# An encoder on one core: sums of down weights beside the output projection, operands kept and stored later, the residual stream in DRAM, another cast order

## The chip, the core and the metric

The kernel runs on one core of a Trainium2 chip. The core has five engines that run at the same time, each through its own list of instructions in order: TensorE (PE, matrix multiplies into PSUM, with its weight loads shown as PEld), VectorE (DVE), ScalarE (ACT), GpSimd (POOL) and SyncE (SP), which issues all the DMAs of this kernel. SBUF is the on-chip memory, PSUM holds the sums of matmuls, and DRAM holds inputs, outputs and scratch. Engines wait for each other by semaphores. The metric is the device time of one execution in microseconds (us); less is better.

## The reference

Two sequences, a prompt of 256 tokens and a sample of 512, go through the same two-layer encoder of width 1024. The first layer mixes with an mLSTM that runs in both directions, the second with sliding-window attention; each is followed by an FFN whose hidden rows are convolved along the sequence.

```python
def conv_ffn(h, w_up, conv_w, conv_b, w_down):
    u = h @ w_up
    u = lax.conv_general_dilated(u, conv_w[:, None, :], ...) + conv_b
    g = u[..., :D_FF]
    val = u[..., D_FF:]
    return (jax.nn.silu(g) * val) @ w_down

def trunk(x, c, ...):
    for l in range(DEPTH):
        mod = jax.nn.silu(c) @ adaln_w[l] + adaln_b[l]
        sh1, sc1, g1, sh2, sc2, g2 = ...
        h = rmsnorm(x, norm_g[l, 0]) * (1 + sc1) + sh1
        y = mlstm_mixer(...) if l % N_MIXERS == 0 else swa_mixer(...)
        x = x + g1 * y
        h = rmsnorm(x, norm_g[l, 1]) * (1 + sc2) + sh2
        x = x + g2 * conv_ffn(h, ffn_w_up[l], ffn_conv_w[l], ffn_conv_b[l], ffn_w_down[l])
    return rmsnorm(x, final_g)
```

D_FF is 2816. Everything is in float32.

## The kernel before

**Layout.** Both sequences stand side by side as T = 768 columns (the prompt first), with the 1024 features on 8 blocks of 128 partitions. `xt` is the residual stream: two tiles of 128 x 4 x 768. The columns are also cut into two halves of H = 384.

**Precision.** Each float32 operand is split into a rounded high part and the rest: ACT casts (`whi`, L263), DVE subtracts (`wlo`, L264). A product then takes three matmuls: high by high, high by low, low by high. `split` does this for a weight tile of 128 x 1024, `fp_copy_split` for an activation.

**Buffers.** Weights land in `raw` tiles of 128 x 1024, of which there are 5; the two parts go to 3 `whi` and 3 `wlo`. Large tiles ("slabs", some 12 KB per partition) come from one pool of 6: `xt` takes two, and so do the rows of the FFN (`urows`). Small activations come from 8 `nt` tiles. `ps` and `pa` are the two sets of four PSUM banks.

**Order.** A scheduler places the instructions of each engine when the kernel is built, by their order in the program and a simulated timeline; each engine and the DMA queue of SP then run their lists in order. In places the order of PE (and in `head` of ACT and DVE) is the written one. `issue_after(ins)` keeps what follows behind `ins` on the engine of `ins`. Generators are stepped to weave side work into a stage: `self.step(gen, n)`.

**Stages.** `first` and `mlstm` run the first mixer, with the adaLN products of both layers beside it (`fill`, `fillp`). `out_proj` multiplies by the mixer's output weights, 16 tiles of 24 matmuls each (8 blocks of features for each of the two halves), adds to `xt`, squares for the norm and starts `combined`, which normalizes and forms the FFN's inputs. Then `ffn`: `prepare` (3 weight tiles) and `head` (4 more, the first part) overlap the end of `out_proj`. `swa` is the second mixer; then `out_proj` and `ffn` again.

**FFN.** The 22 blocks of hidden features are worked as 11 parts of two pairs each. A pair (`pair`, called from `up`) multiplies a 2 x 2 block matrix by a 2 x 2 block of inputs with seven products instead of eight (Strassen's method in Winograd's form). It loads two weight tiles `ra` and `rb`, POOL forms sums of their quarters in place (L1211 to L1223), three splits `wa`, `wc`, `wb` follow, and PE runs seven groups of 12 matmuls, among them T2 (with `wc`) and T3 (with `wb`). Before T2 the partial product of the first group is copied from one PSUM bank to another (L1227, "the fork"), before T3 again (L1238). `conv` and `silu` follow on ACT and DVE.

**Down projection.** Parts 2 to 9 (SOLO = 2, NBLK = 8) don't multiply by their down weights at once: `operands` makes seven combinations of the 2 x 2 blocks of their output (POOL L1510, DVE L1513 to L1516) in a slab and stores it to `yd` in DRAM. `blocked` then runs the seven products over all eight parts together, step by step; `ready` loads the operands (L1301) and weights (L1305) of a step, casts them into `nt` tiles, and PE multiplies (L1337 to L1339). Three of the steps take the down weights as they are, apart from the halves; the other four take sums of quarters, which `sums(l)` has made before on POOL and stored in `sd`: eight units per layer, each of two loads, four POOL operations (L1266, L1268, L1270, L1273) and two stores (L1271, L1274), in five steps of its generator. Layer 0's sums are stepped in `mlstm`, layer 1's in `swa`, one step for each block of the attention.

**Attention.** For each block POOL scales the softmax rows (L1004) before PE transposes them (L1012).

## Time and profile before

| What | Value |
|---|---|
| Time, median of 3 runs | 1923.91 us (1922.31 to 1925.93) |
| The profiled execution | 1919.72 us, its span 1917.9 us |
| Busy share of the span: PE, DVE, ACT, POOL | 93%, 72%, 50%, 31% |
| Mean granted TensorE clock | 0.972 |
| DMA | 274.69 MB, mean 143 GB/s |
| Chain that ended last, by engine | PE 62%, DVE 13%, DMA 11%, ACT 5%, POOL 4%, issue 4% |

The profile shows one execution. A row of an engine's timeline begins with its start and its length in us, then engine, line, operation, output and input tiles; the bracket at its end is the idle time just before it on that engine and what ended it. A row of a group ends with its count, its busy time and the mean in ns, then idle time and releasers. A row of a list of waits gives total us, times and the longest. Matmuls overlap, so their lengths are longer than the distance of their starts. A DMA row of the page gives how many, KB each, and the median us from issue to landing.

### The profile page before, as it was taken

How to read it: one execution, taken by the hardware profiler on the slowest of the kernel's cores; microseconds unless marked ns; L12 is line 12 of the kernel's file. 1: busy time of each engine (PE TensorE's matmuls, PEld its weight loads, DVE VectorE, ACT ScalarE, POOL GpSimd, SP SyncE). 2: the span in 40 equal slices, each digit the busy share in tenths (PEclk: the TensorE clock that was granted, in tenths of full speed). 3: DMA queues.
4: the chain of work that ended last, by engine and by line, in shares of the span. 5: the costliest groups of instructions: out<-in, count | busy, mean ns of one | idle time of the engine just before them, and what ended most of it. 6: DMA issues, size and time to landing. Idle time of an engine off the chain costs nothing.

```text
span 1917.9 us, 29330 instructions
## 1 busy us (share of the span) xinstructions
PE 1789.0 (93%) x11098; PEld 1677.8 (87%) x11098; DVE 1372.9 (72%) x2077; ACT 953.8 (50%) x1935; POOL 594.2 (31%) x482
## 2 busy tenths in 40 slices
PE   6998979999999999989799989999999999897997
PEld 3977858888998999989799988889989989897997
DVE  4756647777689777777657766666898777776565
ACT  3443414443556445555454556664564455554543
POOL 2115141012014454644200237430135455542001
PEclk8999989999999999999899999999999999998999
DMA  8347676446412233232664346424122232335641
GB/s 327 108 162 232 227 245 240 156 151 215 129 52 78 67 112 106 95 124 95 207 219 156 130 157 226 136 82 130 55 89 67 95 124 95 102 103 201 227 143 66
DMA packets 101177, 274.69 MB, mean 143 GB/s; under 512 B 8279, under 2 KB 40279, under 8 KB 98988
## 3 DMA queue, kind: packets, MB, share of 16 engines
q1 hardware_dynamic: 101036, 272.82, 42.3%
q8 instruction: 87, 1.43, 0.3%
q14 instruction: 54, 0.44, 0.1%
HBM read 227.55 MB, written 45.23 MB: 142 GB/s over the span
## 4 chain that ended last, share of the span: by engine, by line
PE 62%; DVE 13%; DMA 11%; ACT 5%; POOL 4%; issue 4%; SPq 0%; POOLq 0%; ACTq 0%; DVEq 0%
PE ps L257 20%; PE pa L257 9%; PE ps L1178 6%; PE ps L1179 6%; PE ps L1181 6%; DMA raw<-in_w_dram 5%; DMA raw<-in_adaln_w_dram 3%; DVE wlo L264 3%; PE pa L1338 2%; PE pa L1339 2%; PE pa L1337 2%; PE ps L1339 2%; PE ps L1337 2%; PE ps L1338 2%; DVE ada L509 2%
## 5 line engine op out<-in xcount | busy, mean ns | idle before, releaser
L264 DVE TENSOR_TENSOR wlo<-raw,whi 128x1024 fp32r<-128x1024 f32 x261 | 350.9, 1347 | 125.5 <-ACT whi L263 125.0
L263 ACT CAST whi<-raw 128x1024 fp32r<-128x1024 f32 x261 | 272.5, 1047 | 236.1 <-PE ps L1179 54.7
L1178 PE MATMUL ps<-zh,whi 128*128 128x384 f32 x504 | 175.4, 348 | 34.7 <-ACT ps L1227 32.3
L257 PE MATMUL ps<-zh,whi 128*128 128x256 f32 (+1 forms) x560 | 192.3, 344 | 9.7 <-ACT whi L263 9.5
L257 PE MATMUL ps<-zh,wlo 128*128 128x256 f32 (+1 forms) x560 | 187.7, 337 | 8.1 <-DVE wlo L264 8.1
L257 PE MATMUL ps<-zl,whi 128*128 128x256 f32 (+1 forms) x560 | 188.2, 338 | 0.1
L1179 PE MATMUL ps<-zl,whi 128*128 128x384 f32 x504 | 173.4, 344 | 0.8 <-DVE zl L1135 0.8
L1181 PE MATMUL ps<-zh,wlo 128*128 128x384 f32 x504 | 172.9, 343 | 0.0
L509 DVE SCALAR_TENSOR_TENSOR ada<-raw,silc,ada 128x1024 f32<-128x1024 f32 x84 | 116.3, 1418 | 26.7 <-DMA raw<-in_adaln_w_dram 26.7
L1178 PEld LDWEIGHTS ps<-zh,whi 128*128 128x128 f32 x504 | 97.5, 193 | 42.8 <-ACT ps L1227 38.8
L257 PE MATMUL ps<-slab,whi 128*128 128x384 f32 x512 | 132.2, 340 | 0.9 <-DVE slab L264 0.5
L257 PEld LDWEIGHTS ps<-zh,whi 128*128 128x128 f32 x560 | 109.9, 197 | 23.7 <-ACT whi L263 10.4
L1483 ACT ACTIVATE slab<-slab,cstt 128x772 f32<-128x772 f32 x88 | 91.0, 1035 | 78.1 <-DVE slab L1251 76.3
L1211 POOL TENSOR_TENSOR raw<-raw 128x512 f32<-128x512 f32 x40 | 61.2, 1531 | 217.1 <-DMA raw<-in_w_dram 206.4
L1485 DVE SCALAR_TENSOR_TENSOR slab<-slab,cstt,slab 128x771 f32<-128x771 f32 x88 | 106.4, 1210 | 30.1 <-ACT slab L1483 29.9
L257 PEld LDWEIGHTS ps<-zh,wlo 128*128 128x128 f32 x560 | 109.3, 195 | 18.9 <-DVE wlo L264 9.2
L257 PEld LDWEIGHTS ps<-zl,whi 128*128 128x128 f32 x560 | 109.7, 197 | 14.1 <-issue 4.6
L1510 POOL TENSOR_TENSOR slab<-slab 128x512 f32<-128x512 f32 x64 | 92.8, 1471 | 58.8 <-DVE slab L1486 41.4
L263 ACT CAST nt<-slab 128x384 fp32r<-128x384 f32 x112 | 56.8, 512 | 108.4 <-PE pa L1338 61.5
L264 DVE TENSOR_TENSOR nt<-slab,nt 128x384 fp32r<-128x384 f32 x112 | 60.7, 554 | 67.3 <-ACT nt L263 67.3
L1337 PE MATMUL pa<-nt,whi 128*128 128x384 f32 x256 | 87.9, 343 | 21.1 <-ACT nt L263 21.1
L1181 PE MATMUL ps<-yh,wlo 128*128 128x384 f32 x304 | 104.7, 344 | 1.9 <-DVE wlo L264 1.9
(316 smaller groups left out, 5156.2 us busy)
## 6 DMA issues: line engine op xcount, KB each, us to landing
raw<-in_w_dram SPq DMA_DIRECT2D x232, 512.0 KB, 4.0
raw<-in_adaln_w_dram SPq DMA_DIRECT2D x84, 512.0 KB, 5.0
yd<-slab SPq DMA_DIRECT2D x16, 1344.0 KB, 5.3
slab<-yd SPq DMA_DIRECT2D x28, 768.0 KB, 6.2
sd<-raw SPq DMA_DIRECT2D x32, 512.0 KB, 3.9
raw<-sd SPq DMA_DIRECT2D x32, 512.0 KB, 3.8
slab<-in_x_dram SPq DMA_DIRECT2D x12, 512.0 KB, 7.4
slab<-in_adaln_w_dram SPq DMA_DIRECT2D x12, 512.0 KB, 10.4
```

Of the source, the lines that this page charges most:

```text
L257: self.nc.tensor.matmul(out, lhsT, rhs, start=start, stop=stop)
L263: nc.scalar.copy(hi, src)
L264: return nc.vector.tensor_tensor(lo, src, hi.bitcast(F32), ALU.subtract)
L509: stt(acc[:, s], row, w, acc[:, s], ALU.mult, ALU.add)
L1178: mm(o, wh[:, k], hi[k], start=start and k == 0, stop=False, skip_group_check=True)
L1179: mm(o, wh[:, k], lo[k], start=False, stop=False, skip_group_check=True)
L1181: mm(o, wl[:, k], hi[k], start=False, stop=k == 3, skip_group_check=True)
L1337: mm(o[c], wh[:, cs], yh, start=start and k == 0, stop=False, skip_group_check=True)
L1338: mm(o[c], wh[:, cs], yl, start=False, stop=False, skip_group_check=True)
L1483: nc.scalar.activation(y, u, AF.Identity, bias=cb, scale=w(1))
L1485: stt(y[:, 1:], u[:, :-1], w(0), y[:, 1:], ALU.mult, ALU.add)
L1510: nc.gpsimd.tensor_tensor(row[:, p0:p1], yrow[:, 2 + j, b], yrow[:, j, b], ALU.mult)
```

## The change

```diff
@@ out_proj
             norms[z].square(c)
+            self.step(self.fills, 3)
             if i % KC == KC - 1:
@@ mlstm
                     if h:
                         self.step(self.fillp)
-                        self.step(self.fills, 5)
@@ swa
-        extra = self.sums(1)
...
-                if x > 1:
-                    next(extra, None)
...
-        for _ in extra:
-            pass
@@ pair
         wc = self.split(ra)
-        wb = self.split(rb)
         e, b = bank(1), bank(2)
-        nc.scalar.copy(b, fork)
+        fork = nc.scalar.copy(b, fork)
+        with self.tc.issue_after(fork.ins):
+            wb = self.split(rb)
@@ blocked, ready
-            ys = self.slab([P, NBLK, H])
+            ys = self.slab([P, NBLK - 1, H])
             for k in K[::4]:
-                nc.sync.dma_start(ys[:, k : k + 4], yd[k : k + 4, :, z].rearrange("k p t -> p k t"))
+                e = min(k + 4, NBLK - 1)
+                nc.sync.dma_start(ys[:, k:e], yd[k:e, :, z].rearrange("k p t -> p k t"))
+            ys = [ys[:, k] for k in K[:-1]] + [self.final[:, z]]
@@ blocked
                 ready(j)
+            if i == 0:
+                xt[:] = self.load_x(xf)
@@ operands
-            nc.sync.dma_start(yd[k], s)
+            if k == NBLK - 1:
+                self.final = s
+                return
+            return lambda: nc.sync.dma_start(yd[k], s)
@@ up
+                        then = [held.pop()] if held else []
...
+                        if i and stores:
+                            then.append(stores.pop())
...
-                        self.pair(pool, u0 + 3 * p + i, bank, rows, p == 1, held.pop() if held else None)
+                        self.pair(pool, u0 + 3 * p + i, bank, rows, p == 1, lambda: [f() for f in then])
...
-                operands(yrow, p - SOLO)
+                stores.extend(filter(None, [operands(yrow, p - SOLO)]))
@@ ffn
                 down(*prev)
+            if p == SOLO:
+                xf = self.dp.tile([P, KC, T], F32, name=f"xf{l}")
+                for rng in RANGES:
+                    self.save_x(xt, xf, rng)
@@ block
             xt = self.load_x((self.io["x"], xs)[l])
+            self.fills = self.sums(l)
```

- `sums(l)` is stepped in `out_proj` of its own layer, three of its steps after each of the 16 tiles, and no longer in `mlstm` and `swa`.
- In `pair`, ACT's cast for `wb` comes behind the first fork copy L1227.
- `operands` returns its store, and the next part's second pair issues it in the place where it runs the held `silu`, behind the second fork copy L1238. The eighth part's operands stay in their slab (`self.final`) and are neither stored nor loaded.
- After part 2's `up` and the `down` of part 1, `xt` is stored to DRAM (`save_x`, six DMAs of 512 KB), and its two slabs go back to the pool. `blocked` loads it again (`load_x`, six DMAs) after the loads of its first two steps.

More of the change, by code (lines that the diff above doesn't have):

```diff
@@ L1275, in sums, with blocked @@
             yield
-    def blocked(self, l, xt, u, yd):
+    def blocked(self, l, xt, u, yd, xf):
         nc = self.nc
@@ L1307, in ready @@
                 y = [self.tmp([P, H], R) for _ in range(2)]
-                self.fp_copy_split(*y, ys[:, k])
+                self.fp_copy_split(*y, ys[k])
                 parts[i, k] = [t[:, 512 * (k % 2) : 512 * (k % 2 + 1)] for t in wt], y
@@ L1478, in ffn @@
         behind = []
+        stores = []
         def conv(u, y, ch):
@@ L1499, in product @@
                 self.fp_copy_split(g[:, 0, j], g[:, 1, j], y)
-        yd = self.dp.tile([NBLK, P, 7, H], F32, name=f"yd{l}")
+        yd = self.dp.tile([NBLK - 1, P, 7, H], F32, name=f"yd{l}")
         def operands(yrow, k):
@@ L1600, in ffn @@
                 down(*prev)
+            if p == SOLO:
+                xf = self.dp.tile([P, KC, T], F32, name=f"xf{l}")
+                for rng in RANGES:
+                    self.save_x(xt, xf, rng)
             prev = (p, g) if g is not None else None
-        self.blocked(l, xt, u0 + 3 * SOLO + 2, yd)
+        self.blocked(l, xt, u0 + 3 * SOLO + 2, yd, xf)
         down(*prev)
@@ L1651, in first @@
         self.fill = self.adaln_v(1, pool)
-        self.fills = self.sums(0)
         act = self.mlstm(pool, gates, xt)
-        for _ in chain(self.fillp, self.fill, self.fills):
+        for _ in chain(self.fillp, self.fill):
             pass
```

## The prediction

> **What bounds the kernel now.** I read a table of stages first (span, then busy time of each engine with its instructions, granted clock, DMA share, GB/s).
>
> ```profile
> core 0: us, PE busy (x) PEld busy (x) DVE busy (x) ACT busy (x) POOL busy (x), PEclk, DMA share, GB/s
> 105.00:290.00 185.00, 160.31 (x1050) 132.50 (x1050) 114.13 (x182) 66.97 (x176) 60.66 (x40) 0.93 0.68 228
> 290.00:438.00 148.00, 144.77 (x1014) 126.08 (x1013) 116.39 (x191) 66.96 (x174) 19.00 (x14) 1.00 0.54 184
> ...
> 1110.00:1300.00 190.00, 181.93 (x1475) 166.06 (x1474) 122.12 (x363) 115.23 (x361) 96.29 (x128) 0.98 0.47 156
> 716.00:918.00 202.00, 186.95 (x1017) 184.69 (x1016) 153.32 (x146) 106.35 (x180) 104.79 (x73) 0.96 0.31 104
> 1536.00:1737.00 201.00, 187.10 (x1024) 184.90 (x1023) 152.52 (x147) 106.35 (x180) 105.02 (x73) 0.97 0.31 105
> 932.00:949.00 17.00, 6.07 (x24) 5.35 (x23) 11.52 (x14) 7.38 (x13) 5.04 (x2) 0.70 0.85 295
> ```
>
> The stages are: the mLSTM while the sums of layer 0 run beside it (105 to 290), the rest of it without them (290 to 438), the attention with the sums of layer 1 (1110 to 1300), the middle parts of the two FFNs (716, 1536), and the start of the blocked down projection (932). TensorE (PE) is busy nearly all the time, so a gain can only come from its idle time, 24.7, 3.2, 8.1, 15.1, 13.9 and 10.9 us here, and from stretches where the clock falls. The list of its waits (total, times, longest) names two causes:
>
> ```profile
> PE ps L1178 <- ACT ps L1227: 32.3, 16, 3.3
> PE pa L1337 <- ACT nt L263: 21.1, 2, 10.6
> ```
>
> **The sums leave the mLSTM.** One long wait of that stage, in order of time on PE, ACT, SP's queue and POOL:
>
> ```profile
> 248.12 0.80 PE L257 MATMUL ps<-zh,whi 128*128 128x512 f32 x1 [5.05 <-ACT whi L263]
> ...
> 247.03 1.04 ACT L263 CAST whi<-raw 128x1024 fp32r<-128x1024 f32 x1 [4.72 <-DMA raw<-in_w_dram]
> ...
> 239.34 2.85 SPq L272 DMA_DIRECT2D raw<-in_w_dram  x3
> ...
> 245.90 1.26 POOL L1266 TENSOR_TENSOR raw<-raw 128x512 f32<-128x512 f32 x1 [4.54 <-DMA raw<-in_w_dram]
> ```
>
> Three loads go out together: two are for the sums (POOL's L1266 starts when they land), and the third is the projection's weight, cast 1.1 us later. The weight is late because the sums hold two of the five `raw` buffers and go ahead of it on SP's queue. At the control stretch's idle share (3.23/148, 2.2%) the 185 us would have 4.0 us idle, so 20.7 are the sums'. The clock of 0.93 is 13 us of clock, 26 us at half speed; I estimate that waits cover about 11 of these, which leaves 15 x 0.5 = 7.5. Ceiling 28; I take 24, as the DVE chain of adaLN with its own loads stays. Ends: 12 (the next wait takes half) and 33 (all idle and most of the clock).
>
> **They leave the attention.** There POOL works in order:
>
> ```profile
> 1147.85 1.26 POOL L1266 TENSOR_TENSOR raw<-raw 128x512 f32<-128x512 f32 x1 [7.82 <-DMA raw<-in_w_dram]
> 1149.19 1.26 POOL L1268 TENSOR_TENSOR raw<-raw,raw 128x512 f32<-128x512 f32 x1
> 1150.43 0.94 POOL L1004 TENSOR_SCALAR t<-t,st 128x256 f32<-128x256 f32 x2
> ...
> 1150.96 0.47 PE L1012 MATMUL pa<-kct,t 128*128 128x128 f32 x1 [5.02 <-POOL t L1004]
> ```
>
> The scaling L1004, for which PE's transposes wait, stands behind two sum operations, the first of which waits 7.8 us for its load. Without them the 5.0 us go; 0.02 x 190 = 3.8 us of clock go at least by half, and 1 us of smaller waits: 8 in all, ends 4 and 10.
>
> **They arrive at the output projections.** Each has eight units; a unit is two loads, four POOL operations, two stores:
>
> ```profile
> L1273 POOL TENSOR_TENSOR raw<-raw,raw 128x512 f32<-128x512 f32 x16 | 26.5, 1658 | 0.0
> L1270 POOL TENSOR_TENSOR raw<-raw 128x512 f32<-128x512 f32 x16 | 24.3, 1518 | 0.8
> L1268 POOL TENSOR_TENSOR raw<-raw,raw 128x512 f32<-128x512 f32 x16 | 21.5, 1342 | 0.9
> L1266 POOL TENSOR_TENSOR raw<-raw 128x512 f32<-128x512 f32 x16 | 21.3, 1333 | 104.4 <-DMA raw<-in_w_dram 94.5 <-PE ps L257 6.6 <-issue 3.3
> ...
> raw<-in_w_dram SPq DMA_DIRECT2D x232, 512.0 KB, 4.0
> ...
> sd<-raw SPq DMA_DIRECT2D x32, 512.0 KB, 3.9
> ```
>
> and the stage that receives those of layer 0, whole, and its second half with the FFN's `head` (layer 1 has the same shape):
>
> ```profile
> 472.00:540.00 68.00, 68.00 (x399) 68.00 (x398) 45.35 (x79) 32.38 (x57) 2.36 (x4) 1.00 0.43 139
> ...
> 506.00:575.00 69.00, 68.04 (x400) 66.08 (x398) 57.98 (x102) 39.96 (x84) 8.86 (x9) 1.00 0.20 62
> ```
>
> POOL gets 93.6/2 = 46.8 us in a stage of 68 where it now works 2.4: room. DMA gets 32 x 0.52 = 16.8 MB on top of 68 us x 139 GB/s = 9.5 MB. By the rows' own ratios (139 at a share of 0.43, 228 at 0.68) a full share is about 330 GB/s, so the 26.3 MB take 80 us: the sums must start some 12 us before the stage or end after it. An early start is open to them, as they depend on nothing there. The price is buffers. One unit takes 4.0 + 5.9 + 3.9 = 13.8 us and holds two of five `raw`; two at a time make 55 us, one at a time 110. Behind them in program order come the next weights, the three loads of `prepare` and the four of `head`, and POOL's power L155 of both norms waits behind a sum operation. PE has no wait here now, so this can only lose. I take +5 us per layer, one wait as in the mLSTM, +10 in all; ends 0 and +84 (the rival below).
>
> The Trainium skill, SBUF — State Buffer, section "SBUF: two separate sides", speaks against this move: GpSimd and a VectorE operation with two SBUF inputs take turns on one port pair, and the loser waits out the whole instruction. The rows agree in kind:
>
> ```profile
> L264 DVE TENSOR_TENSOR nt<-slab,nt 128x384 fp32r<-128x384 f32 x112 | 60.7, 554 | 67.3 <-ACT nt L263 67.3
> ...
> L1516 DVE TENSOR_TENSOR slab<-slab 128x384 f32<-128x384 f32 x16 | 24.1, 1507 | 0.0
> ```
>
> The same size costs DVE 0.55 us with POOL idle and 1.51 beside POOL's operations. Thirty-two POOL operations could so cost DVE up to 32 x 0.95 = 30 us per layer; it has 68 - 45.35 = 22.7 to spare. I count nothing for it in the sum and keep it as a rival.
>
> **Cast order.** The middle of an FFN part, at one of the 16 waits:
>
> ```profile
> 783.81 1.05 ACT L263 CAST whi<-raw 128x1024 fp32r<-128x1024 f32 x1 [4.75 <-POOL raw L1215]
> 786.31 1.03 ACT L1483 ACTIVATE slab<-slab,cstt 128x772 f32<-128x772 f32 x1 [1.45 <-DVE slab L1251]
> 787.25 1.03 ACT L263 CAST whi<-raw 128x1024 fp32r<-128x1024 f32 x1
> 788.18 0.53 ACT L1191 COPY slab<-ps 128x128 f32<-128x128 f32 x2
> 788.61 0.49 ACT L1227 COPY ps<-ps 128x384 f32<-128x384 f32 x1
> ...
> 784.12 1.65 DVE L1516 TENSOR_TENSOR slab<-slab 128x384 f32<-128x384 f32 x1
> 785.68 0.54 DVE L1251 TENSOR_TENSOR slab<-ps,nt 128x384 f32<-128x384 f32 x1
> 786.15 1.21 DVE L264 TENSOR_TENSOR wlo<-raw,whi 128x1024 fp32r<-128x1024 f32 x1
> ...
> 789.15 0.44 PE L1178 MATMUL ps<-zh,whi 128*128 128x384 f32 x1 [2.16 <-ACT ps L1227]
> ```
>
> PE starts T2 when the copy L1227 ends (789.10). The cast at 787.25 is `wb`; moved behind, the copy comes 1.03 us earlier (0.94 by the starts). What is next late: `wlo` of `wc` ends at 787.36, so the wait can lose 1.8 us at most, and only if the copy also passes the evictions and L1483; it cannot pass L1251, which reads the bank it overwrites (786.22). `wb` comes later, but T3 needs it 24 matmuls after T2, 24 x 186.95/1017 = 4.4 us, and cast plus low part take 1.03 + 1.21. The 16 waits hold 32.3 us, nearly all in the two stages; 16 casts would be 16.5, but some waits hold less than one: 13. Clock: 0.04 x 202 + 0.03 x 201 = 14 us; the wait of 2.16 was followed by a first matmul of 0.44 us where the 10.57 below has 0.69. With waits of about 1 us I take half of it, 7. Together 20; ends 3 (another releaser steps in) and 43 (all).
>
> **The store behind the copy** is one DMA per part. Now it waits on SP for L1516, but the next loads wait longer, for the `raw` that `wlo` frees at 787.36; so 0, ends 0 and 3, the latter inside the 43. The slab stays in use some 20 us longer; the two freed by the residual cover that.
>
> **Last operands kept, residual in DRAM.** The start of the blocked part:
>
> ```profile
> 935.89 9.41 SPq L1301 DMA_DIRECT2D slab<-yd  x6
> ...
> 943.27 0.92 ACT L263 CAST nt<-slab 128x384 fp32r<-128x384 f32 x2
> ...
> 943.83 0.69 PE L1337 MATMUL pa<-nt,whi 128*128 128x384 f32 x1 [10.57 <-ACT nt L263]
> ```
>
> The first operand is loaded only at 935.89, when the last part's rows release a slab, and cast when it lands. With `xt` out of the way two slabs are free some 20 us earlier and the last block needs no trip to DRAM, so both loads can land before PE gets there. I leave 2 us, as ACT and DVE are still at the last part's convolution: 8.5 off, and of the clock (0.30 x 17 = 5.1 us, 10.2 at half, of which 4.4 after the wait) 2: 10 per layer, 20 in all; ends 4 and 26. Cost of the residual: six stores after `down(1)` on SP, ahead of the next pairs' loads, and six loads at the blocked start:
>
> ```profile
> slab<-xs SPq DMA_DIRECT2D x6, 512.0 KB, 7.5
> ```
>
> The stores run at a DMA share of 0.31. The loads wait for the last part's slabs, SP's later weight loads stand behind them, and the first adds need them a step later (2 x 96 matmuls x 0.184 = 35 us after the start): hidden by those matmuls; without that cover six loads at the 7.5 of the row are at most 15 us. I take +2 per layer for SP, +4; ends 0 and +30.
>
> **The sum.** -24 - 8 + 10 - 20 - 20 + 4 = -58 against the profiled execution's 1919.7: 1861.7. The three timed runs' median stands 4.2 above it, so 1866.
>
> **Rivals.**
> One: the output projection runs out of buffers. Only two `raw` are left for the sums, the units go one by one, 8 x 13.8 = 110 us in a stage of 68, and `head`'s loads come behind: 42 us per layer. 1919.7 - 72 + 84 + 4 = 1935.7, with the 4.2 about 1940, slower. It decides from about 34 us per layer. For it: in the mLSTM the units took 20 us each. Against: POOL is free here and the loads may start early. Chance 0.14.
> Two: waits change hands. `wlo` ends as late as the copy, and the blocked start waits for loads queued on SP behind the residual: -24 - 8 - 3 - 4 + 14 = -25, so 1899. For it: `wlo` at 787.36 and DMA share 0.85. Chance 0.18.
> Three: the copy goes right behind L1251 and the half-clock stretches vanish: 15 more there, 9 more in the mLSTM and 5 off the projections' loss: 1837. Chance 0.12.
> Four: POOL and DVE take turns; the sums fall into the second half of the projection, each costs DVE 0.95 us, 30 - 11 of room there = 19 per layer in place of 5: -58 + 28 = -30, so 1894. That is the skill's rule above. Chance 0.08.
> The forecast: 0.48.
>
> **Numbers.** The likeliest case's own range is 1840 to 1892 (the terms' ends do not all fall together). The range, 1832 to 1915, takes in cases two, three and four and leaves out the serial case. What a measurement can tell from no change is 0.2%, some 4 us. Faster: cases but the first, less the tail of two: 0.83; same 0.03; slower 0.14.
>
> **What would show it.** Stage 105 to 290: idle PE under 10 us and clock near 1.00, else the first term is wrong. Attention: no PE wait on L1004 over 1 us. Projections: PE waits on `whi`, on a raw load or on L155 where there are none now; over 30 us in a layer is rival one. FFN middle: waits of L1178 on L1227 down to about 15 us in total; if L1181 waits for `wlo` instead, rival two. Blocked start: L1337's wait at 2 us, not 10. The prediction fails if loads of `raw` in the projections end later than `head` needs them.

## The result, and the profile after

| | before | after |
|---|---|---|
| Time, median (range) | 1924.86 us (1922.31 to 1925.93, 4 runs) | 1906.98 us (1904.59 to 1909.98, 4 runs) |
| Ratio to before, 95% interval | | 0.991 (0.9891 to 0.9929) |
| The profiled execution | 1919.72 us | 1909.98 us, its span 1908.2 us |
| Mean granted clock | 0.972 | 0.970 |

The kernel is faster, by 18 us or 0.9%, which the interval sets clear of no change; forecast were 58 us. The table of stages of the kernel after, with the same columns as in the prediction. The first, second and fourth rows are the mLSTM and the attention, which no longer hold sums, the third is the first output projection, which now does, the fifth and sixth are the middle parts of the two FFNs, the last is the start of the blocked stage (the later stages are shifted by as much as they come earlier):

```profile
105.00:290.00 185.00, 179.30 (x1288) 151.81 (x1288) 123.48 (x227) 81.23 (x219) 10.65 (x8) 0.99 0.54 177
290.00:438.00 148.00, 146.21 (x948) 126.05 (x946) 113.98 (x165) 60.14 (x146) 27.90 (x20) 1.00 0.51 169
440.00:536.00 96.00, 80.28 (x421) 75.98 (x420) 55.77 (x82) 35.02 (x61) 51.57 (x37) 0.91 0.82 284
1100.00:1290.00 190.00, 184.64 (x1492) 168.53 (x1493) 126.36 (x376) 120.24 (x373) 73.92 (x112) 0.98 0.36 112
710.00:912.00 202.00, 191.04 (x1050) 188.02 (x1050) 159.76 (x152) 110.03 (x185) 111.83 (x76) 0.97 0.31 107
1526.00:1727.00 201.00, 189.29 (x1045) 185.52 (x1045) 158.95 (x151) 108.90 (x184) 112.16 (x76) 0.98 0.31 107
925.00:942.00 17.00, 6.08 (x22) 5.36 (x21) 11.68 (x14) 7.37 (x13) 5.03 (x2) 0.60 0.89 299
```

The mLSTM's idle time fell from 24.7 to 5.7 us and its clock came back to 0.99. The blocked start did not move at all: 6.08 us busy of 17, as before. And a stage that had no idle time now has 15.7 us of it at a clock of 0.91. The list of PE's waits over the whole span says the same:

```profile
PE ps L1173 <- ACT ps L1221: 22.0, 14, 2.6
PE pa L1337 <- ACT nt L263: 21.2, 2, 10.6
PE ps L257 <- ACT whi L263: 16.0, 12, 3.2
...
PE ps L1176 <- DVE wlo L264: 4.9, 5, 2.2
```

(L1173 and L1221 are the lines that were L1178 and L1227.) The wait for the copy of the running sum fell from 32.3 to 22.0 us, the wait at the blocked start is unchanged, and the wait of the mixers' and projections' matmuls (L257) for a weight's cast grew from 9.8 to 16.0 us, of which 12.6 lie in the first output projection, which had none.

To compare kernels stage by stage I use the time from the first matmul of a stage to the first of the next in each kernel's profiled execution, in us. "mLSTM" is all up to the first output projection, "start" the gap from an FFN's last quarter to the first blocked matmul, "attention" the time from the last blocked matmul of layer 0 to the end of the second projection. Both projections are taken to the start of their last matmul, 0.2 us before the next stage.

| kernel | mLSTM | proj. 0 | FFN 0 | start 0 | attention, proj. 1 | FFN 1 | start 1 |
|---|---|---|---|---|---|---|---|
| before | 468.2 | 70.2 | 394.3 | 10.9 | 296.2 | 392.7 | 10.9 |
| after | 440.9 | 94.8 | 390.2 | 10.9 | 292.4 | 393.2 | 11.0 |
| sums back | 473.3 | 70.2 | 388.7 | 10.9 | 299.9 | 388.0 | 10.9 |
| cast order alone | 465.5 | 70.2 | 386.3 | 10.9 | 296.6 | 388.3 | 10.9 |
| remaining edits alone | 463.5 | 70.2 | 394.0 | 10.9 | 301.2 | 394.6 | 10.9 |
| casts behind, alone | 440.2 | 95.5 | 390.3 | 0.2 | 291.1 | 389.2 | 0.2 |
| loads ahead, alone | 441.0 | 94.5 | 391.9 | 11.7 | 291.3 | 389.8 | 11.7 |
| both at the start | 440.9 | 91.9 | 391.4 | 0.2 | 292.4 | 393.9 | 0.2 |
| no stores of sums | 439.4 | 81.0 | 391.4 | 10.9 | 289.2 | 389.2 | 10.9 |
| a sixteenth stored | 440.7 | 81.9 | 392.6 | 10.9 | 292.0 | 390.1 | 10.9 |
| stores on POOL's queue | 438.6 | 105.5 | 389.9 | 10.9 | 292.0 | 390.4 | 10.9 |
| sums spread | 447.5 | 84.9 | 392.2 | 10.9 | 291.4 | 392.1 | 10.9 |
| sums in mLSTM, step by step | 467.5 | 70.3 | 387.3 | 11.0 | 292.0 | 390.0 | 10.9 |
| sums 0 in the FFN | 440.7 | 70.2 | 414.7 | 0.2 | 293.7 | 391.4 | 0.2 |
| adds behind | 437.9 | 92.4 | 386.4 | 0.2 | 293.0 | 381.3 | 0.2 |

Four rows (before, sums back, cast alone, remaining edits alone) run the mLSTM with the same code and differ by 9.8 us there, so a single pair of profiles does not measure that stage to better than that. The nine rows that hold no sums there differ by 3.1 us.

### The profile page after: what moved, and what is told of

Its sections match the earlier page's. It is cut to its first block, busy times and chain, and to the rows that moved or that the text cites. A ratio compares the mean times of both kernels' runs of the same rounds, so it can differ in the third digit from the quotient of the medians.

```text
span 1908.2 us, 29324 instructions
## 1 busy us (share of the span) xinstructions
PE 1793.6 (94%) x11098; PEld 1679.8 (88%) x11098; DVE 1378.4 (72%) x2077; ACT 955.4 (50%) x1935; POOL 602.6 (32%) x482
## 4 chain that ended last, share of the span: by engine, by line
PE 44%; DVE 13%; POOL 5%; issue 5%; ACT 5%; DMA 4%; POOLq 0%; SPq 0%; DVEq 0%; ACTq 0%
PE pa L257 7%; PE ps L257 6%; PE ps L1173 6%; PE ps L1176 5%; PE ps L1174 5%; DMA raw<-in_w_dram 3%; DVE wlo L264 3%; PE pa L1338 2%; PE pa L1339 2%; PE pa L1337 2%; PE ps L1338 2%; PE ps L1337 2%; PE ps L1339 2%; ACT whi L263 2%; DVE slab L1486 2%
## 5 line engine op out<-in xcount | busy, mean ns | idle before, releaser
L1173 PE MATMUL ps<-zh,whi 128*128 128x384 f32 x504 | 172.7, 343 | 22.4 <-ACT ps L1221 22.0
L257 PE MATMUL ps<-zh,whi 128*128 128x256 f32 (+1 forms) x560 | 189.6, 340 | 2.5 <-ACT whi L263 1.9
L257 PE MATMUL ps<-zh,wlo 128*128 128x256 f32 (+1 forms) x560 | 185.1, 332 | 2.0 <-DVE wlo L264 2.0
L257 PE MATMUL ps<-zl,whi 128*128 128x256 f32 (+1 forms) x560 | 185.5, 333 | 0.0
L257 PE MATMUL ps<-slab,whi 128*128 128x384 f32 x512 | 137.8, 351 | 14.6 <-ACT whi L263 14.1
L1484 ACT ACTIVATE slab<-slab,cstt 128x772 f32<-128x772 f32 x88 | 91.0, 1034 | 113.2 <-DVE slab L1247 112.2
L1486 DVE SCALAR_TENSOR_TENSOR slab<-slab,cstt,slab 128x771 f32<-128x771 f32 x88 | 114.7, 1305 | 35.4 <-ACT slab L1484 35.3
L257 PEld LDWEIGHTS ps<-zh,whi 128*128 128x128 f32 x560 | 107.8, 193 | 16.1 <-issue 4.4
L1173 PEld LDWEIGHTS ps<-zh,whi 128*128 128x128 f32 x504 | 95.6, 190 | 29.0 <-ACT ps L1221 26.8
L509 DVE SCALAR_TENSOR_TENSOR ada<-raw,silc,ada 128x1024 f32<-128x1024 f32 x84 | 110.2, 1349 | 14.8 <-DMA raw<-in_adaln_w_dram 14.8
L1511 POOL TENSOR_TENSOR slab<-slab 128x512 f32<-128x512 f32 x64 | 97.5, 1544 | 66.7 <-DVE slab L1487 54.7
L257 PEld LDWEIGHTS ps<-zh,wlo 128*128 128x128 f32 x560 | 107.5, 192 | 12.4 <-DVE wlo L264 2.9
L257 PEld LDWEIGHTS ps<-zl,whi 128*128 128x128 f32 x560 | 107.6, 193 | 12.1 <-issue 3.4
L257 PEld LDWEIGHTS ps<-slab,whi 128*128 128x128 f32 x512 | 95.1, 195 | 18.6 <-ACT whi L263 17.3
L1176 PE MATMUL ps<-yh,wlo 128*128 128x384 f32 x304 | 105.5, 347 | 4.7 <-DVE wlo L264 4.5
```

Of the source, the lines that this page charges most:

```text
L257: self.nc.tensor.matmul(out, lhsT, rhs, start=start, stop=stop)
L509: stt(acc[:, s], row, w, acc[:, s], ALU.mult, ALU.add)
L1173: mm(o, wh[:, k], hi[k], start=start and k == 0, stop=False, skip_group_check=True)
L1176: mm(o, wl[:, k], hi[k], start=False, stop=k == 3, skip_group_check=True)
L1484: nc.scalar.activation(y, u, AF.Identity, bias=cb, scale=w(1))
L1486: stt(y[:, 1:], u[:, :-1], w(0), y[:, 1:], ALU.mult, ALU.add)
```

## The experiments

### The change taken apart

**Sums back.** Layer 0's and layer 1's sums go back to the mLSTM and the attention, the rest of the change stays:

```diff
@@ out_proj
-            self.step(self.fills, 3)
@@ mlstm
+                        self.step(self.fills, 5)
@@ swa
+        extra = self.sums(1)
...
+                if x > 1:
+                    next(extra, None)
```

> The kernel after, with the sums of both layers put back where they stood before (12 units of the mLSTM heads, the attention loop); the rest of the change stays. Theory A, from the two traces' stretches: the move of the sums took 27.3 us out of the stretch ahead of the first output projection and 5.0 us out of the attention, and put 24.7 us into the first output projection and 2.1 us into the second, so it is worth about 5.5 us: 1912 us here (1909 to 1916), with the first output projection back at about 70 us. Rival, the prediction's own terms (24 and 8 us gained, 10 us lost): the move is worth 22 us, 1929 us here.

Measured: 1915.07 us (1911.43 to 1920.59, 6 runs), ratio 0.9948 (0.9928 to 0.9967). The move of the sums is worth 1915 - 1907 = 8 us, near theory A and far from the 22 of the prediction's terms.

**Cast order alone**, on the kernel before:

```diff
         wc = self.split(ra)
-        wb = self.split(rb)
         e, b = bank(1), bank(2)
-        nc.scalar.copy(b, fork)
+        fork = nc.scalar.copy(b, fork)
+        with self.tc.issue_after(fork.ins):
+            wb = self.split(rb)
```

> The kernel before with one edit alone: the cast of the second raw tile stands behind the first copy of the running sum. The prediction's term: 20 us less, 1905 us. Theory A: the copy is released earlier, but the weight's low half and the sum row that the next quarters need end at nearly the old time, so that only a few us are left: 1918 to 1924 us, with the waits of the first quarter for the row of the running sum at about 22 us in place of 32.

Measured: 1909.88 us (1904.98 to 1913.18), ratio 0.9916 (0.9891 to 0.9942). That is 16 us below the runs of before beside it (1926.05 us), as much as the whole change brings; 12.4 of them are in the two FFNs (8.0 and 4.4) and the rest in the mLSTM, whose code is the same, within its scatter. It lies below theory A's range, which fails, and 5 us above the 1905 of the prediction's term.

**The remaining edits alone**: the store behind the copy, the last operands kept, the residual stream in DRAM; sums and cast order as before (the two diffs above reversed in the kernel after).

> The kernel before with the remaining edits alone: operands stored behind the next part's copy, the last ones kept, the residual stream in DRAM between. Sums and cast order stay as before. The prediction's term: the blocked stage starts 10 us sooner in each layer, less 4 us for SyncE: 1908 to 1910 us. Theory A (the start is set by the last part's product casts, which these edits don't touch, and the FFN's parts 2 and 3 grew by 2.5 and 1.0 us beside the kernel with the cast order alone): the idle time ahead of the first blocked matmul stays at 10.6 us, and the time is 1922 to 1930 us.

Measured: 1924.84 us (1921.52 to 1930.49, 10 runs), ratio 1.0011 (0.9998 to 1.0023). Nothing: these edits neither gain nor cost a measurable time, and the start stays at 10.9 us.

### What holds the start of the blocked stage

The timeline of the kernel after, by engine, at that start (ACT, POOL, SP's queue, PE):

```profile
932.17 0.83 ACT L263 CAST slab<-slab 128x772 fp32r<-128x772 f32 x1 [3.32 <-POOL slab L1499]
935.70 0.83 ACT L263 CAST slab<-slab 128x772 fp32r<-128x772 f32 x1 [2.69 <-POOL slab L1499]
936.44 1.75 ACT L263 CAST nt<-slab 128x384 fp32r<-128x384 f32 x4
...
929.67 2.47 POOL L1499 TENSOR_TENSOR slab<-slab 128x772 f32<-128x772 f32 x1 [16.86 <-ACT slab L1484]
933.10 2.57 POOL L1499 TENSOR_TENSOR slab<-slab 128x772 f32<-128x772 f32 x1 [0.96 <-ACT slab L263]
...
929.06 2.66 SPq L1298 DMA_DIRECT2D slab<-yd  x4
...
937.00 0.69 PE L1337 MATMUL pa<-nt,whi 128*128 128x384 f32 x1 [10.56 <-ACT nt L263]
```

Two things end together at 936.2 to 936.5: the operand load, issued only at 929.06 and landed 7.1 us later (a slab was free before, as the next runs show), and on ACT the two casts of the last part's product, which wait for POOL's multiplications (929.67 and 933.10) and stand ahead of the first operand cast. Three kernels tell them apart.

```diff
@@ up                                  (casts behind)
-            elif p:
+            elif p == NPART - 1:
+                self.last = lambda: product(yrow, g)
+            elif p:
                 product(yrow, g)
@@ blocked
                 ready(j)
+                if j == 0:
+                    self.last()
```

```diff
@@ blocked                             (loads ahead)
+        first = [stored(i) for i in (0, 1)]
...
+                    with self.tc.issue_after(first[1][2]):
-                    nc.sync.dma_start(raw, src(k).rearrange("k p c -> p k c"))
+                        nc.sync.dma_start(raw, src(k).rearrange("k p c -> p k c"))
```

Here `stored(i)` is the part of `ready(i)` that takes a slab and loads the operands into it. Both moves in one:

> The kernel after with two moves at the start of the blocked stage: the loads of the first two operand groups are issued ahead of the blocked stage's weight loads, and the last part's product casts stand behind the first operand group on ScalarE. Theory A (the late operand load and the product casts ahead of the first operand cast end within 1 us of each other, so that neither alone is the bound): the idle time of 10.6 us ahead of the first blocked matmul falls under 4 us in both layers, 1907 minus 13 = 1894 us (1890 to 1899). Rival (another thing holds the first matmul, such as the last part's evictions or the low halves on VectorE): the idle time stays over 8 us and the time at 1903 to 1910 us.

Measured: 1884.69 us (1880.85 to 1889.4), ratio 0.9789 (0.9759 to 0.9818). The gap is 0.2 us in both layers, and the time 9 below the value that theory A gave. The loads alone:

> The kernel after with only the loads of the first two operand groups issued ahead of the blocked stage's weight loads; the product casts stay where they are. Theory A (two constraints that end together, load and casts): the product casts, which wait for GpSimd's products until 933 to 936 us, still stand ahead of the first operand cast on ScalarE, so the idle time ahead of the first blocked matmul stays at 8 to 10.6 us and the time at 1903 to 1908 us. Rival (the late load alone): the idle time falls under 3 us and the time comes to within 3 us of the kernel with both moves, 1885 to 1889 us.

Measured: 1908.4 us (1902.12 to 1909.4), ratio 0.9914 (0.9891 to 0.9936): no gain over the kernel after. The timeline of SP's queue and of ACT, where the row at 935.75 is the second product cast:

```profile
922.30 2.31 SPq L1296 DMA_DIRECT2D slab<-yd  x4
...
935.75 0.83 ACT L263 CAST slab<-slab 128x772 fp32r<-128x772 f32 x1 [2.69 <-POOL slab L1507]
936.49 1.75 ACT L263 CAST nt<-slab 128x384 fp32r<-128x384 f32 x4
```

The load now goes out 6.8 us sooner and has landed at 926.9, and the first operand cast still begins at 936.49, right behind the second product cast. The casts alone:

> The kernel after with only the last part's product casts moved behind the first operand group; the operand loads stay behind the weight loads. Theory A: the operand load still lands late, so the idle time stays, 1903 to 1908 us, or more where the first operand casts, now ahead of the last part's work on ScalarE, hold that work up as well. Rival (the casts alone): the idle time falls under 3 us, 1885 to 1889 us.

Measured: 1881.67 us (1878.45 to 1882.54), ratio 0.9778 (0.9761 to 0.9796). Theory A's picture of two equal constraints falls: one edit takes the whole gap (21.5 of the 25 us are the two gaps). The same two engines there:

```profile
902.54 1.01 SPq L1298 DMA_DIRECT2D slab<-yd  x2
...
922.73 1.34 ACT L263 CAST nt<-slab 128x384 fp32r<-128x384 f32 x3
...
933.04 0.84 ACT L263 CAST slab<-slab 128x772 fp32r<-128x772 f32 x1
```

With the casts out of the way the scheduler itself put the first operand load at 902.54, ahead of the weight loads. In the kernel after it was late because its only reader was planned late: the late load was a symptom. The product casts now run at 933 among the blocked matmuls, where nothing waits for them.

### What the sums cost where they run

Beside the waits for `whi`, the first output projection of the kernel after moves 27 MB (this row is the transfers between 440 and 536 us):

```profile
DMA packets 8616, 27.22 MB, mean 284 GB/s; under 512 B 832, under 2 KB 2368, under 8 KB 8610
```

**No stores.** The two `dma_start` of `sums` are left out, and `summed(i)` reads what `given(i)` reads.

> The kernel after with the sums loaded and added as before but not stored; the blocked stage reads the weights themselves in their place, so as many bytes are loaded there. 8.4 MB less are written in each output projection. Theory B (the first output projection is crowded by transfers, 27 MB in 95 us): it falls from 95 us to about 78 us, and the time to about 1889 us. Rival C (the five raw buffers are held by the loads and adds, not by the bytes): less than 6 us of it goes, 1901 to 1907 us.

Measured: 1889.54 us (1888.65 to 1896.31), ratio 0.9832 (0.9805 to 0.9859). The projection takes 81.0 us:

```profile
439.00:520.00 81.00, 74.55 (x412) 72.57 (x411) 52.09 (x78) 33.38 (x59) 50.88 (x37) 0.96 0.70 230
```

POOL works as long as it did with the stores (50.88 against 51.57 us), idle PE fell from 15.7 to 6.5 us and the clock rose to 0.96.

**A sixteenth stored**, so that the order and the waits stay:

```diff
-            nc.sync.dma_start(sd[k, :, :1024], r[0])
+            nc.sync.dma_start(sd[k, :, :64], r[0][:, :64])
...
-            nc.sync.dma_start(sd[k, :, 1024:], r[1])
+            nc.sync.dma_start(sd[k, :, 1024:1088], r[1][:, :64])
```

> The kernel after with a sixteenth of the stores' bytes: 64 of 1024 columns of every tile of sums are stored, in the same order and with the same waits; the blocked stage reads the weights themselves in place of the sums. Theory B (bytes): the first output projection stays within 3 us of the 81 us that it took with no stores, 1888 to 1892 us. Rival G (the store's place in the order and the time until the buffer is free, which has a part that doesn't shrink with bytes): it is back at 88 us or more, 1896 to 1907 us.

Measured: 1897.55 us (1896.32 to 1898.7), ratio 0.9869 (0.9853 to 0.9886). The projection itself is at 81.9 us, within the bound set for bytes, and rival G's 88 is out. So it is the stores' bytes that cost: a store of 32 KB still takes 4.1 us from issue to landing, against 4.4 for 512 KB, and stands at the same place in the order. The median does not agree: it lies in G's range, 8 us above the run with no stores. By the stages 3 of these lie in the attention and second projection and the others are scattered; I read the projection, and leave the rest open.

**Stores on POOL's queue** (`nc.gpsimd.dma_start` in place of `nc.sync.dma_start`):

> The kernel after with the stores of the sums issued from GpSimd's own queue, right behind its adds, in place of SyncE's queue, where weight loads stand behind stores that wait for adds; the bytes and the buffers are the same. Theory B (bytes): no change of the first output projection beyond 4 us, 1903 to 1911 us. Rival D (order in SyncE's queue): the first output projection falls to about 80 us, 1892 us.

Measured: 1916.88 us (1913.18 to 1926.45, 10 runs), ratio 0.9968 (0.9953 to 0.9982); the projection takes 105.5 us. The gain of rival D did not come; things got worse. In the projection, the DMA row of the stores reads

```profile
sd<-raw POOLq DMA_DIRECT2D x16, 512.0 KB, 6.0
```

The Trainium skill (Trainium Kernel Development and Optimization, section "Key Constraints") says that transfers issued from different engines share the same 16 DMA engines and only the time of issuing is saved; the runs agree that nothing was gained. A store took 4.4 us from SP's queue in the kernel after (median of the 16 in this projection) and 6.0 here, and the 16 issues themselves take 9.2 us on POOL, so this run changes more than the order in SP's queue.

What the stores hold shows in that queue. It waits before a load (L272) until a store has landed and its `raw` is free; the totals in this projection, in the kernel after, with a sixteenth stored and with POOL's queue:

```profile
SPq L272 <- DMA sd<-raw: 21.4, 12, 4.1
...
SPq L272 <- DMA sd<-raw: 8.8, 6, 2.1
...
SPq L272 <- DMA sd<-raw: 46.0, 15, 6.6
```

The loads land after 5.7, 4.9 and 5.9 us (4.3 before the change, 4.7 with no stores). Busier DMA engines and buffers that are held thus go together in all of these runs, and none of them separates the two.

**Spread**: 16 of layer 0's steps ride in the mLSTM's output gate stage, the projection takes 2 steps a tile (`self.step(self.fills)` behind each `gemmT` of that stage).

> The kernel after with layer 0's sums begun earlier: 16 of their 40 steps ride in the mLSTM's output gate stage, one behind each group of matmuls, and the output projection takes 2 steps a tile in place of 3; layer 1 as after. Theory B (the first output projection is crowded by transfers: the DMA engines are busy 0.8 to 0.93 of the time between 440 and 520 us): with a third of the sums' transfers gone ahead, the projection falls from 95 us to about 82 us, and the gate stage, at a DMA share of 0.5 to 0.75, gives back at most 4 us: 1895 to 1900 us. Rival (each unit of the sums costs about 3 us wherever it runs, through the five raw buffers or the adds on GpSimd): what the projection gains the gate stage loses, 1904 to 1910 us.

Measured: 1907.04 us (1905.26 to 1907.24), ratio 0.9901 (0.9882 to 0.9921): the projection gained 9.9 us and the mLSTM lost 6.6; the rival is right. **Step by step** in the mLSTM, 24 steps in the heads and 16 in the gate stage:

> The kernel after with layer 0's sums back in the mLSTM, but one of a unit's five steps at a time (24 behind the groups of matmuls of the heads 1 to 3, 16 in the output gate stage) where before they ran five steps at once; layer 1 as after. Theory H (a unit costs some 3 us wherever it runs, 2 us a unit in the gate stage of the earlier run): the stretch to the first output projection is back near 463 to 468 us and the projection at 70 us, 1905 to 1911 us. Rival I (five steps at once made the loss in the mLSTM, because its adds stand ahead of the heads' own work on GpSimd): the stretch stays under 452 us, 1885 to 1895 us.

Measured: 1911.94 us (1906.86 to 1914.2), ratio 0.9939 (0.9919 to 0.9959). Up to the projection 467.5 us, as with five steps at once: theory H's range there, with the median 1 us above its range of times. **In the FFN**, on the kernel with the casts behind, five steps behind each of the parts 1 to 8 in place of the projection:

> The kernel with the product casts behind the first operand group (1882 us) and layer 0's sums in its FFN in place of its first output projection: a unit behind each of the parts 1 to 8; layer 1 as after. There the DMA engines are busy a third of the time and GpSimd about 0.55 of it. Theory B (bytes): the first output projection is back at 70 us, and the FFN gives back less than that: 1860 to 1870 us. Rival (GpSimd's adds stand ahead of the pairs' own sums, and five raw buffers are shared with their loads): the FFN gives back 3 us or more a unit, 1880 us or above.

Measured: 1878.69 us (1874.66 to 1882.08), ratio 0.9765 (0.9741 to 0.9789). The projection is back at 70.2 us and the FFN of layer 0 takes 24.4 us more than in the kernel it was built on, 3 us a unit: the rival, though the median is 3 us below that kernel, within their ranges. The first of PE's waits in that FFN (10.7 us in the kernel it was built on):

```profile
PE ps L1174 <- ACT ps L1222: 18.5, 5, 4.4
```

### What is left of the FFN's wait

One of the seven waits of a layer in the kernel after, on DVE, ACT and PE:

```profile
843.18 1.07 DVE L1514 TENSOR_TENSOR slab<-slab 128x384 f32<-128x384 f32 x1 [1.19 <-POOL slab L1511]
...
847.30 1.64 DVE L1517 TENSOR_TENSOR slab<-slab 128x384 f32<-128x384 f32 x1
848.86 0.54 DVE L1247 TENSOR_TENSOR slab<-ps,nt 128x384 f32<-128x384 f32 x1
...
849.49 1.03 ACT L1484 ACTIVATE slab<-slab,cstt 128x772 f32<-128x772 f32 x1 [7.07 <-DVE slab L1247]
850.43 1.03 ACT L263 CAST whi<-raw 128x1024 fp32r<-128x1024 f32 x1
851.36 0.53 ACT L1186 COPY slab<-ps 128x128 f32<-128x128 f32 x2
851.78 0.49 ACT L1221 COPY ps<-ps 128x384 f32<-128x384 f32 x1
...
852.32 0.44 PE L1173 MATMUL ps<-zh,whi 128*128 128x384 f32 x1 [1.98 <-ACT ps L1221]
```

ACT stood idle for 7 us ahead of the convolution L1484, which waits for the row sum L1247, which stands on DVE behind four operand adds; the copy that PE waits for comes fourth. A first try moved the convolutions of a part's second pair, and the operand adds after them, behind the next pair's copy:

> The kernel after with the product casts behind the first operand group (as in the run with that alone, 1882 us) and, in the parts between, the convolutions and operand adds of a part's second pair behind the next pair's first copy of the running sum. Theory E: what is left of the wait of the first quarter for that copy (2 us a part, and the half clock that follows some of them) is the convolution ahead of the copy on ScalarE, which itself waits for VectorE's row sum behind four operand adds; without it a part takes 29.5 to 30.5 us in place of 31.3 to 33.7 and the FFN 375 to 380 us in place of 390 to 393: 1854 to 1864 us. Rival F (the weight's low halves on VectorE, or the row sum itself, are late next): less than 1 us a part, 1874 to 1882 us.

Measured: 1906.99 us (1905.97 to 1908.61), ratio 0.9918 (0.9903 to 0.9933), 25 us worse than the kernel it was built on (1882). It moved the wrong pair: behind the copy that it freed PE had not been waiting. The copy of a part's second pair is still late, and later than before (37.4 us of waits in place of 22.3). One of these waits, on DVE, ACT and PE (L1522 is the last operand add there, L1250 the row sum, L1489 the convolution, L1222 the copy):

```profile
889.27 1.64 DVE L1522 TENSOR_TENSOR slab<-slab 128x384 f32<-128x384 f32 x1
890.84 0.54 DVE L1250 TENSOR_TENSOR slab<-ps,nt 128x384 f32<-128x384 f32 x1
...
891.47 1.03 ACT L1489 ACTIVATE slab<-slab,cstt 128x772 f32<-128x772 f32 x1 [8.04 <-DVE slab L1250]
...
893.90 1.03 ACT L1489 ACTIVATE slab<-slab,cstt 128x772 f32<-128x772 f32 x1
894.84 0.47 ACT L1222 COPY ps<-ps 128x384 f32<-128x384 f32 x1
...
895.36 0.62 PE L1174 MATMUL ps<-zh,whi 128*128 128x384 f32 x1 [3.85 <-ACT ps L1222]
```

The row sum still stands behind the operand adds, and both convolutions of the first pair, no longer one, now stand ahead of the copy.

Then the right pair, the adds, and both, each on the kernel with the casts behind:

```diff
@@ up                                  (convolutions of the first pair)
-                for j in range(2):
-                    conv(urow[:, 2 * i + j], yrow[:, 2 * i + j], i * FC + 2 * p + j)
+                if i == 0 and p >= SOLO:
+                    self.late.append(rows_of)
+                else:
+                    rows_of()
@@ pair
             wb = self.split(rb)
+            while self.late:
+                self.late.pop(0)()
```

```diff
@@ operands                            (adds behind)
+            def adds():
...
+            self.adds.append(adds)
@@ pair
+        row = nc.vector.tensor_tensor(r1[:, col(H) :], b, p5, ALU.add)
...
+        while self.adds:
+            with self.tc.issue_after(row.ins):
+                self.adds.pop(0)()
```

> The kernel with the product casts behind the first operand group (1882 us) and the convolutions of a part's first pair behind the second pair's first copy of the running sum (the run before moved those of the second pair, whose next copy had not been waiting). Theory E1: the 2 us waits for that copy, one a part, come from the convolution ahead of it on ScalarE, which waits for the row sum on VectorE; they fall under 0.7 us and part of the half clock with them: 8 to 14 us a layer, 1854 to 1868 us. Rival F: the weight's low half, which VectorE makes 1 us behind the copy, takes the wait over: 1874 to 1882 us.

> The kernel with the product casts behind the first operand group (1882 us) and the four operand adds of a part behind the next first pair's row sum on VectorE; the convolutions stay where they are. Theory E2: the row sum was late because the adds, slowed from 0.55 to 1.1 to 1.65 us beside GpSimd's adds, stand ahead of it; it comes some 1.5 us earlier, convolution and copy with it, and the waits fall from 2 us to under 1 us: 1862 to 1874 us. Rival F2: the row sum's own quarter is the limit (it is ready only then), 1878 to 1884 us.

> Both of the two runs before in one. If E1 and E2 are two ways to the same wait, no more than 3 us below the better of them; if the copy and the low half are held by one each, the sum of both, 1850 to 1860 us.

| kernel | median (range), us | ratio, 95% interval | PE's waits for the copy, whole span: us, times, longest |
|---|---|---|---|
| casts behind | 1881.67 (1878.45 to 1882.54) | 0.9778 (0.9761 to 0.9796) | 22.3, 14, 2.8 |
| + convolutions of the first pair | 1872.52 (1869.93 to 1876.14) | 0.9735 (0.9711 to 0.9759) | 19.4, 14, 2.0 |
| + adds behind | 1866.07 (1863.36 to 1867.48) | 0.9699 (0.9678 to 0.9719) | 13.9, 11, 1.7 |
| + both | 1866.4 (1862.76 to 1868.62) | 0.9706 (0.9681 to 0.973) | 12.2, 13, 1.7 |

The adds are worth 16 us and the convolutions 9; both together no more than the adds. E1 missed: the waits for the copy hardly shrank, and the time is 4 us above its range. What went with the convolutions was PE's wait for `wlo`, the first line below, from the kernel with the casts behind; neither move alone leaves any of it in the pairs. The second line is the kernel with both moves, where it is back:

```profile
PE ps L1176 <- DVE wlo L264: 7.3, 7, 2.2
...
PE ps L1178 <- DVE wlo L266: 7.2, 12, 0.6
```

Moving the adds also took 8.4 us off the waits for the copy, and 5.6 us came back at the second copy (0.4 to 6.0). So the adds ahead of the row sum were part of what held the copy, and the two edits overlap at `wlo`. E2's time is right, but not its waits of under 1 us; what holds the 13.9 us that are left is open. The kernel with the casts and the adds behind beats both kernels: it is faster than before by 3.0% and than after by 2.1% (1866.07 to 1906.98).

## Why the prediction was right or wrong

Right were the direction, two of its three gains in kind, and two terms in size. **The sums leave the mLSTM**: 24 forecast. The profiled pair shows 27.3; the mean of the four kernels that run them there is 467.6 us, 26.7 above after. **They leave the attention**, 8 forecast, and arrive at the second projection, 5 forecast as a loss: the two together are 298.5 us in the four kernels with sums in the attention and 292.4 after, a gain of 6 where the terms gave 3. Waits on L1004 fell to 2.4 us in two, though the longest, 2.2, is over the 1 us that I set.

**The step that failed is the start of the blocked stage.** I wrote that the first operand is loaded only late "and cast when it lands", and so took 8.5 of the 10.6 us off by freeing slabs, with 2 for the clock: 10 per layer, 20 in all. It gave nothing (remaining edits alone: 1.0011). The quoted row had the answer beside it: the cast at 943.27 stood in ACT's order behind the product's casts, and these behind POOL. I read the releaser of the wait and the landing of the load, and did not ask what stands ahead of the cast on its own engine. These rows of ACT and POOL, from the kernel before, stand just ahead of it:

```profile
942.53 0.83 ACT L263 CAST slab<-slab 128x772 fp32r<-128x772 f32 x1 [2.70 <-POOL slab L1498]
...
939.92 2.57 POOL L1498 TENSOR_TENSOR slab<-slab 128x772 f32<-128x772 f32 x1 [0.96 <-ACT slab L263]
```

That the 20 us were there is shown: with the casts moved 1907 became 1882. The bounds that I set (4 to 26) excluded no gain at all, which was wrong too.

**The sums' arrival at the first projection was mis-sized**: 5 forecast, 24.6 measured in the profiled pair (91.9 to 95.5 us over the kernels with the same code, against 70.2). I had worked out 80 us of transfers for a stage of 68, and then let the sums start early for free. They began only at the stage's edge, and the weights shared the DMA engines with 16.8 MB of sums: without the stores 13.8 us of the loss go, with a sixteenth of their bytes 12.9. The remaining 11 us go with loads and adds; between these two and the five buffers no run decided. Rival one named the stage and the sign, with 42 per layer too large; its buffers had a part, as SP's queue waited 21.4 us there for stores to free them, but how large a part beside the shared DMA engines stays open. Rival four's adds on POOL were the same with and without stores, so they don't explain that part.

**The cast order was mis-sized**: 20 forecast, 16 by the medians of the run alone, 12.4 by its FFNs, and 3.6 in the two FFNs of the profiled kernel after. The waits fell to 22.0 us where I had said about 15. The step that was off is "what is late next": I named `wlo` and bounded the gain there, and rival two took it up, but `wlo` took only 4.9 us in all; late next was the same copy, behind a convolution that waits for a row sum behind the operand adds. The other part of the difference is the clock, which I had at half of 14 us: the table of the two FFNs, of before, after and cast order alone, has

```profile
538.60:932.90 394.30, 372.94 (x2066) 361.64 (x2065) 312.68 (x337) 210.76 (x358) 177.98 (x116) 0.98 0.28 94
1359.00:1751.70 392.70, 372.08 (x2066) 360.77 (x2066) 313.12 (x335) 210.73 (x358) 177.67 (x116) 0.98 0.28 94
```

```profile
535.90:926.10 390.20, 372.45 (x2067) 360.67 (x2066) 317.07 (x338) 212.00 (x358) 179.17 (x116) 0.98 0.30 99
1348.70:1741.90 393.20, 374.48 (x2068) 361.50 (x2066) 319.02 (x336) 211.56 (x359) 182.23 (x119) 0.98 0.30 99
```

```profile
535.90:922.20 386.30, 368.95 (x2067) 357.71 (x2065) 316.60 (x337) 211.80 (x358) 183.16 (x116) 0.99 0.29 96
1348.50:1736.80 388.30, 369.76 (x2067) 357.54 (x2066) 317.06 (x335) 211.44 (x358) 180.08 (x116) 0.99 0.29 95
```

Idle PE fell from 42 us to 36 in both kernels with the new order, but the clock rose only in the second: busy time at a lower clock is 8.2 of the 8.8 us that lie between them. The last section says on what that hangs.

**Residual in DRAM**, +4 forecast: no cost to be measured in the run of the remaining edits, which has it together with the two moves of the operands; on its own it was not run. **The sum**: the blocked start 20 short, the first projection 20, the cast order some 16 in the profiled execution, against 4 for SP and some 4 from the mLSTM and the attention, which did better than forecast: -58 + 56 - 4 - 4 = -10, and the profiled executions have 1909.98 - 1919.72 = -10.

## What to carry to other kernels

A wait that a profile puts down to a cast or a copy may be set by what stands ahead of that instruction on its own engine, so read that engine's order back to the first instruction with an idle bracket before moving its operands sooner; a load that looks late may only be planned late, because its reader is. Work that is moved from a stage with idle PE to one without brings only the difference of the two, and its bytes count there as its instructions do: here layer 0's eight units cost 24 to 27 us in each of three stages. Where two edits might cure one wait, run each alone and both together, and look at which waits each of them took.

## What the runs showed of the hardware

**The clock after a short wait.** In the kernel after, the middle FFN waits alternate between 1.55 and 1.98 us. The clock in the 5 us after one of each, and after the same wait of 1.98 us in the kernel with the sums back:

```profile
787.35 0.44 PE L1173 MATMUL ps<-zh,whi 128*128 128x384 f32 x1 [1.98 <-ACT ps L1221]
...
820.60 0.44 PE L1173 MATMUL ps<-zh,whi 128*128 128x384 f32 x1 [1.55 <-ACT ps L1221]
```

```profile
787.35:792.35 5.00, 5.00 (x19) 4.85 (x20) 4.93 (x6) 3.96 (x6) 0.00 (x0) 0.66 0.67 209
820.60:825.60 5.00, 5.00 (x28) 5.00 (x29) 4.56 (x6) 3.99 (x7) 0.00 (x0) 1.00 0.48 143
```

```profile
794.22:799.22 5.00, 5.00 (x28) 4.86 (x29) 4.92 (x6) 3.89 (x6) 0.00 (x0) 1.00 0.65 221
```

0.66 over 5 us is 3.4 us at half clock, 1.7 us lost, and 19 matmuls in place of 28: a wait of 1.98 us costs 1.98 or 3.7. In the FFNs of after, cast order alone, sums back and step by step, all 32 waits for the copy from 1.54 to 1.69 us were followed by full clock; of the 16 from 1.98 to 2.84 us the eight in the first two kernels were followed by half clock and the eight in the others, at the same places of the program, were not. The Trainium skill (TensorE: Matmul & The Clock Gate, section "Why this matters for your kernels") asks for no idle gap over about 3 us; here less than 2 was enough. The Trainium skill's section "What's actually happening" of that page says that the activity window runs free of the kernel and is 3.4 us long, which fits the length and the chance, though no run here moved the phase on purpose. This is a good part of why the FFN with the new cast order took 386 to 394 us from kernel to kernel: by the granted clock, the two FFNs spent 31 us at half clock in the kernel after, 14 in cast order alone and 10 in sums back. It is not what the adds' move gained: there the half clock took 14 us of the two FFNs with and without it, and the 11.8 us that they gained are PE's idle time, which fell from 39.8 to 28.7 us. It is no sharp line: once, in the kernel with convolutions and adds moved, half clock followed a wait of 1.28 us.

**A unit of sums cost about 3 us wherever layer 0 ran it**: 26.7 us for the eight in the mLSTM, 24.6 in the projection, 24.4 in the FFN, where the DMA engines are busy 0.31 of the time without the sums and 0.40 with them. In the FFN the cost stands in other waits (those for the copy grew from 10.7 to 18.5 us), so the equal sums may be chance; that was not tried.
